# Hybrid decoder layer on one core: the token-major results and the decay chain get an earlier place in the schedule, and the decay sums become a step of their own

## The chip, the core and the metric

The kernel runs on one NeuronCore of a Trainium2 chip: TensorE (PE, with its weight loads as PEld), VectorE (DVE), ScalarE (ACT), GpSimd (POOL) and SyncE (SP, which issues the loads). Each engine takes its instructions strictly in its own order, and waits on semaphores for the other engines and for DMAs. The metric is the device time of one execution in microseconds; lower is better.

## The reference, cut to what matters

One decoder layer on 512 tokens of width 1024. One input projection feeds two mixers, a sparse attention with three gated branches and a gated DeltaNet (a recurrence with per-head decay); their outputs are merged, projected and normalised, and a convolutional MLP follows.

```
h = x @ w_in[l]
(nsa_q, cmp_k, cmp_v, slc_k, slc_v, win_k, win_v, nsa_gate,
 gdn_qkv, gdn_beta, gdn_decay, gdn_gate, merge_gate) = _split_in(h)
...
beta = jax.nn.sigmoid(beta_raw.astype(f32)).transpose(0, 2, 1)
g = (-jnp.exp(a_log.astype(f32))[None, :, None]
     * jax.nn.softplus(decay_raw.astype(f32) + dt_bias.astype(f32)).transpose(0, 2, 1))
...
gcum = jnp.cumsum(g, axis=-1)
...
mix = (jax.nn.sigmoid(gate_a) * y_a + jax.nn.sigmoid(gate_b) * y_b) @ w_o[l]
x = layer_norm(DEEPNORM_ALPHA * x + mix, ln1_g[l], ln1_b[l])
f = conv_ffn(x, ffn_w_up[l], ffn_conv_w[l], ffn_w_down[l])
x = layer_norm(DEEPNORM_ALPHA * x + f, ln2_g[l], ln2_b[l])
```

All of it is kept in float32: a product is made of three passes over operands split into a high and a low part (high by high, low by high, high by low), which is why nearly every operand has two tiles (`wh` and `wl`, `xh` and `xl`, `kh` and `kl`).

## The kernel before

**The start.** SP loads the transposed input in eight blocks of 128 channels (`xr`) and, beside them, the 288 columns of the input projection that are wanted with tokens on the partitions (`wB`: the values of two attention branches, the attention gates, beta and the decay). ACT and DVE split each block. `token_major` (L299) multiplies them block by block into four accumulators, `pb0` to `pb3`, one for each 128 tokens: 96 matmuls of 128x288. Of these accumulators ACT and DVE then take the values (`vcat`), the gates (`gsig`) and the eight columns of beta and decay (`bd`).

**The steps.** All other columns of the projection are made channel-major in pieces of 128 columns by `gemm_t`: a weight tile of 512 KB (`raw`) is loaded, split in two halves into `wh` and `wl`, and 24 matmuls of 128x512 go into a bank `gps`. There are two banks `gps`, three buffers each for `raw`, `wh` and `wl`, and the block-wise weights of `token_major` use the same `wh` and `wl` buffers. A string, `ORDER` (L128), lists the steps up to the merge. The first are `q0` (queries of the first pair of heads), `k0` (keys of the first group), `i0` (keys of the first recurrent head: product, convolution of four taps, four transposes, norms), `q1`, `j0` (queries of the first recurrent head), `m0` (its matrices) and `c` (the compressed keys and values). In what follows a product is called by its step: "q0's product" is the 24 matmuls into that step's `gps`.

**Evacuation.** `queries` (L679) empties its bank by four ACT and two DVE operations (`q`, `qf`), `keys` (L662) by four ACT (`kh`, L673) and four DVE (`kl`, L675) operations. `conv_silu` (L400) reads the bank with ACT (`acc`, L404), with DVE (L412) and, for the taps that POOL adds, with ACT again (`tap`, L409); only then is the bank free. For i0 two taps go over ACT and POOL, and POOL also makes the last two multiplications (`kq`, L420) ahead of the transposes (L426).

**The decay chain.** `decays` (L361) turns `bd` into beta and into `gdec`, the log decay: ACT makes `tb` and `se`, and DVE some thirty small operations of 128x16, each waiting for the one ahead of it (`sacc`, L382 and L383, is the longest part). Three matmuls (L394) against constant triangles make the cumulated sums, ACT takes their exponential (`eg`), DVE makes `nbe`. `gdh` and `gdl` are the split halves of `gdec` that `m0` wants (`grh`, `grl` on POOL).

**What sets the order.** The instructions are written in program order and given a priority number by a running counter; a list scheduler then sets each engine's order by these numbers and by what it reckons to be ready. `tc.high_priority(offset=n)` makes the numbers inside a block smaller (earlier) by n, and on leaving it the counter stands again where it stood on entering. The steps stand each in such a block, with an offset made of the numbers used so far (`at`) and a shift from the table `SHIFT`. So what stands inside such blocks does not move the number from which the steps count; what stands outside does. Before the change the evacuation of `token_major` and the whole of `decays` stand outside.

## Time and profile before

| | |
|---|---|
| time, median of three runs | 853.08 us (850.83 to 854.49) |
| profiled execution | span 852.4 us, from its first instruction to its last |
| PE busy | 830.1 us, 97% of the span |
| DVE / ACT / POOL busy | 597.5 / 403.6 / 160.9 us |
| mean granted TensorE clock | 0.991 |

The page gives no other time of the profiled execution than its span. A row of the timeline has the start and the length in us, the engine, the line, the operation, output and input tiles without their buffer numbers, and in brackets the idle time before it with what ended it. Matmuls are pipelined, so the distance between the starts of two rows, and not their length, is what one of them costs. "PEclk" is the clock that TensorE was granted, 1.00 being full.

### The profile page before, as it was taken

Reading aid. Unit: us, or ns where it says so; the run is one execution under the profiler, and the core shown is the slowest. Engines: PE = TensorE matmul, PEld = TensorE weight load, DVE = VectorE, ACT = ScalarE, POOL = GpSimd, SP = SyncE. Lnnn points to the kernel's source line nnn. Section 1 sums busy time; section 2 is a strip of 40 time slices with the busy share of each in tenths; the row PEclk is TensorE's granted clock in tenths of the full one; section 3 lists DMA queues with packets and bytes.
Section 4 is the critical chain, followed back from the end, with each engine's and each line's share of the span. In section 5 each row is a group of like instructions: output and inputs, shape, how many; then the busy total and the mean of one; then the engine's idle time right before and its main releaser. Section 6 shows DMA issues by size and latency. Waiting matters only on the chain.

```text
span 852.4 us, 11870 instructions
## 1 busy us (share of the span) xinstructions
PE 830.1 (97%) x4226; PEld 681.5 (80%) x4226; DVE 597.5 (70%) x1276; ACT 403.6 (47%) x890; POOL 160.9 (19%) x152
## 2 busy tenths in 40 slices
PE   8999899999999999999999999999999999999986
PEld 8777688777777788888888898888888888878864
DVE  5845579986867866674457647777777777877686
ACT  4464377575446776532234114444444444655531
POOL 0353442223136111102200003111111111100000
PEclk9999899999999999999999999999999999999998
DMA  7322111002102010254446008997966732565662
GB/s 271 86 92 99 53 48 50 25 26 75 49 27 75 26 50 25 88 181 127 124 152 219 26 1 292 253 244 236 228 206 170 198 99 86 185 210 174 203 192 99
DMA packets 35051, 108.05 MB, mean 127 GB/s; under 512 B 3248, under 2 KB 4400, under 8 KB 34608
## 3 DMA queue, kind: packets, MB, share of 16 engines
q1 hardware_dynamic: 27696, 84.23, 30.9%
q0 software_dynamic: 7296, 23.07, 11.4%
q8 instruction: 33, 0.54, 0.3%
q14 instruction: 26, 0.21, 0.1%
HBM read 105.19 MB, written 25.17 MB: 153 GB/s over the span
## 4 chain that ended last, share of the span: by engine, by line
PE 80%; DVE 11%; DMA 4%; ACT 2%; issue 2%; POOL 0%; SPq 0%; DVEq 0%; ACTq 0%; POOLq 0%
PE pu L264 9%; PE pu L262 9%; PE pu L265 9%; PE gps L262 7%; PE gps L264 7%; PE gps L265 7%; PE pout L851 2%; PE aps L834 2%; DMA raw<-wsum 2%; PE px L1136 2%; PE pw L1014 2%; PE pw L1012 2%; PE pm L265 2%; PE pm L262 2%; PE pw L1013 2%
## 5 line engine op out<-in xcount | busy, mean ns | idle before, releaser
L252 DVE TENSOR_TENSOR wl<-raw,wh 128x512 fp32r<-128x512 f32 x140 | 113.4, 811 | 67.2 <-ACT wh L248 62.8
L248 ACT ACTIVATE wh<-raw 128x512 fp32r<-128x512 f32 x136 | 85.5, 631 | 152.2 <-PE pu L264 104.2
L262 PE MATMUL pu<-mh,wh 128*128 128x512 f32 (+1 forms) x384 | 142.7, 372 | 0.0
L264 PE MATMUL pu<-ml,wh 128*128 128x512 f32 (+1 forms) x384 | 142.6, 371 | 0.0
L265 PE MATMUL pu<-mh,wl 128*128 128x512 f32 (+1 forms) x384 | 142.6, 371 | 0.0
L262 PE MATMUL gps<-xh,wh 128*128 128x512 f32 x320 | 129.7, 407 | 2.5 <-DVE xs L536 2.2
L264 PE MATMUL gps<-xl,wh 128*128 128x512 f32 x320 | 129.7, 406 | 0.0
L265 PE MATMUL gps<-xh,wl 128*128 128x512 f32 x320 | 127.8, 401 | 0.0
L262 PEld LDWEIGHTS pu<-mh,wh 128*128 128x128 f32 x384 | 72.4, 188 | 12.6
L265 PEld LDWEIGHTS pu<-mh,wl 128*128 128x128 f32 x384 | 72.4, 188 | 12.6
L264 PEld LDWEIGHTS pu<-ml,wh 128*128 128x128 f32 x384 | 72.4, 188 | 12.3
L262 PEld LDWEIGHTS gps<-xh,wh 128*128 128x128 f32 x320 | 60.8, 190 | 15.8 <-issue 2.9
L1094 DVE SCALAR_TENSOR_TENSOR fa<-pu,fcw,fa 128x511 f32<-128x511 f32 x88 | 65.7, 746 | 10.7 <-ACT fa L1091 9.2
L264 PEld LDWEIGHTS gps<-xl,wh 128*128 128x128 f32 x320 | 60.9, 190 | 11.0 <-issue 1.0
L265 PEld LDWEIGHTS gps<-xh,wl 128*128 128x128 f32 x320 | 60.9, 190 | 10.9 <-issue 0.2
L1100 POOL TENSOR_TENSOR fth<-fth,fa 128x512 f32<-128x512 f32 x22 | 28.7, 1303 | 201.5 <-DVE fa L1094 201.5
L252 POOL TENSOR_TENSOR wl<-raw,wh 128x512 fp32r<-128x512 f32 x36 | 46.3, 1288 | 93.3 <-ACT wh L248 79.2
L1071 ACT ACTIVATE wh<-raw 128x512 fp32r<-128x512 f32 x67 | 40.6, 627 | 40.9 <-DMA raw<-wsum 16.8
L1072 DVE TENSOR_TENSOR wl<-raw,wh 128x512 fp32r<-128x512 f32 x67 | 43.8, 685 | 21.0 <-ACT wh L1071 20.7
L811 ACT ACTIVATE sc<-sc,mn 128x384 f32<-128x384 f32 (+2 forms) x64 | 35.7, 559 | 12.8 <-DVE mn L809 10.6
L295 POOL TENSOR_TENSOR rs<-rs,minus_half 128x1 f32<-128x1 f32 x8 | 7.6, 946 | 170.3 <-DVE rs L973 170.3
L1091 ACT ACTIVATE fa<-pu,fcw 128x512 f32<-128x512 f32 x44 | 29.6, 672 | 10.2 <-PE pu L265 10.2
(329 smaller groups left out, 1684.0 us busy)
## 6 DMA issues: line engine op xcount, KB each, us to landing
raw<-in_up SPq DMA_DIRECT2D x44, 512.0 KB, 4.5
raw<-in_wT SPq DMA_DIRECT2D x40, 512.0 KB, 3.6
wsum<-in_down POOLq DMA_DIRECT2D x6, 2816.0 KB, 24.3
raw<-wsum SPq DMA_DIRECT2D x20, 512.0 KB, 4.3
raw<-in_down SPq DMA_DIRECT2D x15, 512.0 KB, 4.8
wsum<-wsum POOLq DMA_DIRECT2D x2, 2816.0 KB, 12.5
raw<-in_wm SPq DMA_DIRECT2D x8, 512.0 KB, 3.7
raw<-in_wo SPq DMA_DIRECT2D x8, 512.0 KB, 3.6
```

Of the source, the lines that this page charges most:

```text
L248: A.activation(wh, r, AF.Copy)
L252: eng.tensor_tensor(wl, r, wh.bitcast(F32), op=OP.subtract)
L262: i = PE.matmul(ps, wh[k], mh_(k), start=(k == 0), stop=False)
L264: PE.matmul(ps, wh[k], ml_(k), start=False, stop=False)
L265: PE.matmul(ps, wl[k], mh_(k), start=False, stop=(k == n - 1))
L811: A.activation(s[:, i, :n], s[:, i, :n], AF.Exp, scale=-1.0, bias=mn[:, 0, i:i + 1], accum_out=mn[:, 1, i:i + 1])
L834: PE.transpose(pt[:, i, k, :], s[:, i, k * 128:(k + 1) * 128], ident)
L1071: A.activation(hi, raw[:, i], AF.Copy)
L1072: V.tensor_tensor(lo, raw[:, i], hi.bitcast(F32), op=OP.subtract)
L1091: A.activation(acc, ps, AF.Copy, scale=w[:, 2:3])
L1094: V.scalar_tensor_tensor(acc[:, n:], ps[:, :S - n], w[:, i:i + 1], acc[:, n:], op0=OP.mult, op1=OP.add)
L1100: G.tensor_tensor(th, th, g[1], op=OP.mult)
```

## The change

Three edits. The evacuation of the token-major accumulators moves into a block with priority 600 numbers earlier, and the four copies of `bd` come ahead of the values and gates. `decays` moves into such a block as well, and loses its tail. That tail (the three matmuls of the sums, the exponential and `nbe`) becomes `decay_sums`, a step `d` between `k0` and `i0` without an entry in `SHIFT`. No instruction is added or removed.

```diff
 LATE = 2500
+EARLY = 600
...
-ORDER = "q0 k0 i0 q1 j0 m0 c n0 w0 i1 j1 v0 v1 p0 o0 a0 y0 b0 a1 b1 m1 a2 b2 n1 w1 i2 j2 o1 y1 m2 v2 a3 n2 q2 w2 b3 o2 y2 q3 g0 p1 k1 i3 j3 a4 b4 m3 a5 n3 w3 g1 g2 b5 v3 o3 a6 g3 b6 a7 g4 b7 g5 y3".split()
+ORDER = "q0 k0 d i0 q1 j0 m0 c n0 w0 i1 j1 v0 v1 p0 o0 a0 y0 b0 a1 b1 m1 a2 b2 n1 w1 i2 j2 o1 y1 m2 v2 a3 n2 q2 w2 b3 o2 y2 q3 g0 p1 k1 i3 j3 a4 b4 m3 a5 n3 w3 g1 g2 b5 v3 o3 a6 g3 b6 a7 g4 b7 g5 y3".split()
...
-        for t in range(TT):
-            ps = pss[t]
-            hi = vcat[:, t, :, :, 0, :]
-            src = ps[:, :256].rearrange("p (a b c) -> p a b c", a=2, b=2)
-            A.activation(hi, src, AF.Copy)
-            V.tensor_tensor(vcat[:, t, :, :, 1, :], src, hi.bitcast(F32), op=OP.subtract)
-            A.activation(gsig[:, t, :], ps[:, 256:280], AF.Tanh, scale=0.5)
-            A.activation(bd[:, t, :], ps[:, 280:288], AF.Copy)
-        V.tensor_scalar(gsig, gsig, 0.5, 0.5, op0=OP.mult, op1=OP.add)
+        with tc.high_priority(offset=EARLY):
+            for t in range(TT):
+                A.activation(bd[:, t, :], pss[t][:, 280:288], AF.Copy)
+            for t in range(TT):
+                ps = pss[t]
+                hi = vcat[:, t, :, :, 0, :]
+                src = ps[:, :256].rearrange("p (a b c) -> p a b c", a=2, b=2)
+                A.activation(hi, src, AF.Copy)
+                V.tensor_tensor(vcat[:, t, :, :, 1, :], src, hi.bitcast(F32), op=OP.subtract)
+                A.activation(gsig[:, t, :], ps[:, 256:280], AF.Tanh, scale=0.5)
+            V.tensor_scalar(gsig, gsig, 0.5, 0.5, op0=OP.mult, op1=OP.add)
...
         V.tensor_tensor(gdl, gdec, gdh.bitcast(F32), op=OP.subtract)
+
+    def decay_sums():
         ps = dps()
         gv = gdec.rearrange("p a b -> p (a b)")
...
-    decays()
+    with tc.high_priority(offset=EARLY):
+        decays()
...
-             "i": gdn_k, "j": gdn_q, "v": gdn_v, "m": gdn_mid, "n": gdn_tri, "w": gdn_inv, "y": gdn_gate,
+             "d": decay_sums, "i": gdn_k, "j": gdn_q, "v": gdn_v, "m": gdn_mid, "n": gdn_tri, "w": gdn_inv, "y": gdn_gate,
```

All that the engines' orders show of the change lies in the first 100 us of the program. Three places carry the prediction. Line numbers after the change are higher by one to six.

**SP, the front of the program** (`raw_391` is the weight tile of q0, `xr0` the first input block, `wB0` the first columns). Before:

```order
L1240 UNCONDITIONAL_BRANCH
L214 DMA xr0_122<-in_xT 128x256
L216 DMA wB0_130<-in_wB 128x288
L214 DMA xr0_122<-in_xT 128x256
L214 DMA xr1_123<-in_xT 128x256
```

After:

```order
L1246 UNCONDITIONAL_BRANCH
L242 DMA raw_391<-in_wT 128x1024
L215 DMA xr0_122<-in_xT 128x256
L217 DMA wB0_130<-in_wB 128x288
L215 DMA xr0_122<-in_xT 128x256
```

The load of q0's weights, which stood behind all input blocks, is now the first load of the program, and every input block stands one place later in the queue.

**PE, the end of the token-major product** (`pb3` is the fourth accumulator, `gps_407` and `gps_401` q0's product, `gps_451` and `gps_445` k0's, `gps_497` i0's, before and after). Before:

```order
L265 MATMUL gps_407<-xh_93,wl_405 128x512
L311 MATMUL pb0_118<-wh_279,xl_94 128x288
L309 MATMUL pb1_119<-wh_279,xh_93 128x288
L310 MATMUL pb1_119<-wl_280,xh_93 128x288
L311 MATMUL pb1_119<-wh_279,xl_94 128x288
L309 MATMUL pb2_120<-wh_279,xh_93 128x288
L310 MATMUL pb2_120<-wl_280,xh_93 128x288
L311 MATMUL pb2_120<-wh_279,xl_94 128x288
L309 MATMUL pb3_121<-wh_279,xh_93 128x288
L310 MATMUL pb3_121<-wl_280,xh_93 128x288
L311 MATMUL pb3_121<-wh_279,xl_94 128x288
L262 MATMUL gps_451<-xh_93,wh_443 128x512
```

After:

```order
L263 MATMUL gps_497<-xh_93,wh_493 128x512
L265 MATMUL gps_497<-xl_94,wh_493 128x512
L266 MATMUL gps_497<-xh_93,wl_495 128x512
L312 MATMUL pb3_121<-wh_279,xl_94 128x288
L266 MATMUL gps_445<-xh_93,wl_443 128x512
L263 MATMUL gps_445<-xh_93,wh_441 128x512
L265 MATMUL gps_445<-xl_94,wh_441 128x512
L266 MATMUL gps_445<-xh_93,wl_443 128x512
```

The last token-major matmul, which stood between q0's product and k0's, now stands behind the whole of i0's product, ahead of the last seven matmuls of k0's. The ten token-major matmuls before it are strewn among those of k0 and i0. The three matmuls of the decay sums, which stood among the last three matmuls of k0's product, now stand behind j0's product, round the transposes of i0.

**ACT and DVE, the evacuation of i0 and k0 and the decay chain** (`acc_522`, `tap_525` and `tap_528` empty i0's bank; `wh_602` is the first half of j0's weights; `kh` and `kl` empty k0's bank). ACT before:

```order
L404 ACTIVATE acc_522<-gps_497,tiny_317 128x512
L409 ACTIVATE tap_525<-gps_497,tiny_317 128x510
L409 ACTIVATE tap_528<-gps_497,tiny_317 128x509
L395 ACTIVATE eg_335<-dps_391 128x48
L673 ACTIVATE kh_476<-gps_451 64x512 x2
L248 ACTIVATE wh_602<-raw_600 128x512
```

ACT after:

```order
L409 ACTIVATE acc_522<-gps_497,tiny_317 128x512
L315 ACTIVATE bd_106<-pb3_121 128x8
L320 ACTIVATE vcat_104<-pb3_121 128x4x64
L367 ACTIVATE tb_352<-bd_106 128x16
L249 ACTIVATE wh_602<-raw_600 128x512
L414 ACTIVATE tap_525<-gps_497,tiny_317 128x510
L414 ACTIVATE tap_528<-gps_497,tiny_317 128x509
L375 ACTIVATE se_358<-say_359 128x16
```

DVE before, the end of the chain:

```order
L388 SCALAR_TENSOR_TENSOR gdec_332<-sacc_368,ea_386 128x16
L412 SCALAR_TENSOR_TENSOR acc_522<-gps_497,tiny_317,acc_522 128x511
L389 CAST gdh_333<-gdec_332 128x16
L390 TENSOR_TENSOR gdl_334<-gdec_332,gdh_333 128x16
L396 SCALAR_TENSOR_TENSOR nbe_336<-beta_331,eg_335 128x16
L675 TENSOR_TENSOR kl_477<-gps_451,kh_476 64x512 x2
```

DVE after, the middle of the chain:

```order
L385 TENSOR_TENSOR sacc_368<-sacc_368,sz2_366 128x16
L680 TENSOR_TENSOR kl_471<-gps_445,kh_470 64x512
L386 TENSOR_SCALAR sacc_368<-sacc_368 128x16
L680 TENSOR_TENSOR kl_471<-gps_445,kh_470 64x512
L253 TENSOR_TENSOR wl_604<-raw_600,wh_602 128x512
L385 TENSOR_TENSOR sacc_368<-sacc_368,sz2_366 128x16
```

On ACT the first half of j0's weights moved from behind i0's taps and k0's first copies to ahead of the taps, together with the last `bd` and `vcat`. On DVE the chain was closed before k0's low parts (`kl`) and j0's weights (`wl_604`); now i0's first convolution step stands ahead of the chain, and the chain runs round the `kl` operations and on behind `wl_604`.

## The prediction

> **What bounds the kernel now.** I read the page first, then PE's waits, then the stretches round them.
>
> ```profile
> span 852.4 us, 11870 instructions
> PE 830.1 (97%) x4226; PEld 681.5 (80%) x4226; DVE 597.5 (70%) x1276; ACT 403.6 (47%) x890; POOL 160.9 (19%) x152
> ...
> PE gps L262 <- DVE xs L536: 2.2, 1, 2.2
> PE dps L394 <- DVE gdec L388: 1.6, 1, 1.6
> ...
> PE pb L309 <- ACT wh L233: 1.0, 1, 1.0
> ...
> PE gps L262 <- ACT qf L689: 0.3, 1, 0.3
> ```
>
> PE is busy for 97% of the span, and of its few waits one is the change's target: the matmuls of the decay sums (L394) wait 1.6 us for `gdec`. The stretches show a second cost behind it (columns: stretch, length, busy time and instructions of PE, PEld, DVE, ACT, POOL, granted clock, DMA share, GB/s):
>
> ```profile
> 5.00:9.20 4.20, 3.21 (x24) 2.86 (x22) 1.85 (x4) 1.95 (x5) 0.00 (x0) 1.00 0.91 268
> 9.20:17.00 7.80, 7.67 (x55) 7.33 (x55) 6.38 (x14) 4.82 (x10) 0.00 (x0) 1.00 1.03 402
> ...
> 35.80:38.00 2.20, 0.55 (x4) 0.23 (x3) 1.93 (x10) 0.00 (x0) 0.00 (x0) 1.00 0.00 0
> 38.00:42.30 4.30, 4.30 (x16) 3.20 (x16) 2.87 (x6) 3.17 (x6) 3.93 (x4) 0.62 0.18 23
> ...
> 93.30:100.00 6.70, 6.49 (x25) 5.82 (x26) 1.98 (x4) 2.85 (x5) 3.18 (x3) 0.52 0.01 2
> ```
>
> After the wait the granted clock is 0.62 for 4.3 us, which loses (1 - 0.62) x 4.3 = 1.6 us of PE work. So this wait costs 1.6 + 1.6 = 3.2 us. The wait of 2.2 us for `xs`, which ends at 93.3, is followed by 6.7 us at 0.52, another 3.2 us; the 1.0 us of L309, between 5 and 9.2, costs no clock. So a wait of about 1.6 us is enough to slow the clock, one of 1.0 us is not.
>
> The rows of PE that carry the sum:
>
> ```profile
> 28.60 0.50 PE L262 MATMUL gps<-xh,wh 128*128 128x512 f32 x1 [0.28 <-ACT qf L689]
> ...
> 35.54 0.39 PE L264 MATMUL gps<-xl,wh 128*128 128x512 f32 x1
> 35.77 0.39 PE L265 MATMUL gps<-xh,wl 128*128 128x512 f32 x1
> 37.80 0.37 PE L394 MATMUL dps<-gdec,cst 128*128 128x16 f32 x2 [1.65 <-DVE gdec L388]
> ...
> 38.33 0.29 PE L394 MATMUL dps<-gdec,cst 128*128 128x16 f32 x2
> ...
> 39.60 0.76 PE L262 MATMUL gps<-xh,wh 128*128 128x512 f32 x1
> ...
> 46.91 0.39 PE L265 MATMUL gps<-xh,wl 128*128 128x512 f32 x1
> ...
> 51.91 0.60 PE L426 MATMUL dps<-ident,kq 128*128 128x128 f32 x4
> ...
> 52.81 0.40 PE L265 MATMUL gps<-xh,wl 128*128 128x512 f32 x1
> ...
> 57.69 0.33 PE L426 MATMUL dps<-ident,kq 128*128 128x128 f32 x1
> ```
>
> i0's product begins at 28.60, the sums at 37.80, q1's product at 39.60, the third matmul of j0's product is at 46.91, i0's transposes at 51.91, the third matmul of c's first product at 52.81 and j0's transposes at 57.69. A matmul of 128x512 costs 0.23 us at full clock (35.54 to 35.77).
>
> **Part one: the weight load at the front.** The token-major matmuls need the input blocks as early as they can come.
>
> ```profile
> 0.73 0.39 SPq L214 DMA_DIRECT2D xr<-in_xT  x1
> ...
> 4.01 4.71 DMA wB<-in_wB
> ...
> 16.64 0.36 DVE L250 CAST wh<-raw 128x512 fp32r<-128x512 f32 x1
> ...
> 24.95 0.29 PE L310 MATMUL pb<-wl,xh 128*128 128x288 f32 x1
> 25.08 0.29 PE L311 MATMUL pb<-wh,xl 128*128 128x288 f32 x1
> ```
>
> The chain of waits runs through this start: the columns of the third block, issued at 4.01, land after 4.71 us, at 8.7, and PE waits for their split. Now 512 KB stand ahead of all blocks. At the 402 GB/s of the stretch from 9.2 to 17 they take 524288 / 402000 = 1.3 us; that is the upper bound. The DMA engines were 0.91 busy from 5 to 9.2, so a queue that is never empty can win back at most 9% of the 8.0 us from 0.73 to 8.7, 0.7 us; that gives 0.6 as the lower bound. I take **+1.0**, between them. No gain is possible, as the tile is first read at 16.64, long after it landed in its old place. After 9.2 PE runs without a gap (7.67 of 7.80 us), so the delay is carried on whole.
>
> [...]
>
> **Part two: from i0's product to q1's.** The times below leave the +1.0 out; it is added at the end.
>
> ```profile
> 24.59 1.21 ACT L316 ACTIVATE vcat<-pb 128x256 fp32r<-128x256 f32 x4
> ...
> 34.38 0.69 ACT L404 ACTIVATE acc<-gps,tiny 128x512 f32<-128x512 f32 x1 [3.25 <-PE gps L265]
> 38.24 1.26 ACT L409 ACTIVATE tap<-gps,tiny 128x510 f32<-128x510 f32 x2 [3.17 <-DVE acc L412]
> 39.68 1.19 ACT L673 ACTIVATE kh<-gps 64x512 fp32r<-64x512 f32 x2
> 40.89 0.63 ACT L248 ACTIVATE wh<-raw 128x512 fp32r<-128x512 f32 x1
> ...
> 32.41 1.15 DVE L380 TENSOR_SCALAR sacc<-sz 128x16 f32<-128x16 f32 x1
> ...
> 36.33 0.17 DVE L383 TENSOR_SCALAR sacc<-sacc 128x16 f32<-128x16 f32 x1
> 36.53 0.17 DVE L382 TENSOR_TENSOR sacc<-sacc,sz 128x16 f32<-128x16 f32 x1
> ...
> 40.90 1.38 DVE L675 TENSOR_TENSOR kl<-gps,kh 64x512 fp32r<-64x512 f32 x2 [0.23 <-ACT kh L673]
> ```
>
> i0's start still hangs on the last copy of q0's bank, whose chain is as long as before, so it stays at 28.6. From there PE has 34 matmuls of 0.23 (all 24 of i0, ten of k0) and four token-major ones of 0.13 (24.95 to 25.08): 8.3 us, to 36.9. i0's last matmul is the 29th of these, at 35.1. q1's product takes i0's bank, and its start waits for the taps: ACT does `acc` (0.69, from 35.5), the last `bd`, `vcat` and `tb` (0.30 for one `vcat`, the small ones estimated at 0.2 each), then `wh_602`, whose buffer is freed only by k0's last but one matmul at about 37.0 (0.63), and the two taps (1.26): 38.9. Behind the waiting `wh_602` stand the taps, `se` and `kh`, and PE and DVE wait for them. So PE waits from 37.2 to 38.9, **1.7 us in place of the 1.6** that were there; the new wait is for taps, not for `gdec`. q1 starts 0.7 earlier than the 39.60 of before, since the sums no longer stand ahead of it.
>
> **Part three: to j0's product.** It takes k0's bank and needs all four `kl`, and its third matmul `wl_604`. `kh` begins when ACT is through with the taps and `se`, at 39.2, and the pairs take 1.2 each. Before, four `kl` (0.69 each) ran behind a closed chain. Now ten `sacc` operations of 0.2 and the chain's start stand among them: chain from 39.2 to 41.2 (seven links, with half a microsecond for one as slow as the 1.15 above), two `kl` to 42.8, seven operations to 44.3, two `kl` to 45.9, `wl_604` (about 0.7) to 46.6. PE would have ended q1 at 38.9 + 24 x 0.23 = 44.4 at full clock, or 46.0 after another slow stretch. Either way j0's third matmul is at 46.7 against 46.91: **the 0.7 shrinks to 0.2**, and the slow clock costs nothing there because DVE's chain ends later.
>
> **Part four: i0's transposes and c.**
>
> ```profile
> 38.37 1.05 POOL L487 TENSOR_TENSOR grh<-cst,gdh 128x512 fp32r<-128x512 f32 x1 [3.58 <-DVE gdh L389]
> ...
> 46.90 1.28 POOL L420 TENSOR_TENSOR kq<-th,acc 128x512 f32<-128x512 f32 x1
> 48.12 0.61 POOL L250 CAST wh<-raw 128x512 fp32r<-128x512 f32 x1
> 48.81 1.29 POOL L252 TENSOR_TENSOR wl<-raw,wh 128x512 fp32r<-128x512 f32 x1
> ...
> 57.62 0.16 DVE L459 TENSOR_TENSOR gk<-gk,nbe 128x4 f32<-128x4 f32 x1
> ```
>
> The nine last links of the chain follow `wl_604`, so `gdh` is there at 48.3, ten us later than before. POOL's order now has `grh` and `grl` (1.05 each) ahead of `kq` (1.28): `kq` is done at 51.7, where before it was at 48.2. PE ends j0 at 46.7 + 22 x 0.23 = 51.8, so the transposes stand at 51.9, as before. Then come the three sums, 0.4 us at full clock (they show 0.29 at the slow one), which PE paid earlier before. c's `wh` and `wl` follow `kq` on POOL (0.61 + 1.29): 53.7, and c's third matmul waits 0.3 for it: **53.75 against 52.81, +0.9**. Twenty more matmuls lead to j0's transposes. `grl` is ready at 50.4, well ahead of the matmul behind them; `nbe` comes near 54 and is read at 57.62. Both are hidden with 3 us and more; without that cover the ten us that the chain lost would show.
>
> The values and gates, moved along with `bd`, are first read by the attention steps behind c and cost nothing.
>
> **Sum.** +1.0 + 0.9 = +1.9 on the profiled span: 852.4 + 1.9 = **854.3**. Behind 60 us PE is the bound again and passes the delay on; the wait for `xs` starts and ends with PE's own order. The profiled execution lies 0.7 under the median of 853.08, within the 3.7 us that the runs differ.
>
> **The rivals.** *The change does what it says*: the wait and its slow clock go, no wait comes in their place: 852.4 - 3.2 + 1.0 = 850.2. For it speaks that q1's wait (1.7) stands close to the 1.6 from which the clock is known to fall, and is made of many short rows; against it, that the order has `wh_602` ahead of the taps and the last token-major matmul behind i0. *Slower, by the clock*: the waits at q1 and at j0 each slow the clock after j0 has begun, for as long as the 6.7 us behind the wait for `xs`: +3.2, 857.5. It decides if the second wait comes out at 1.6 or more; my walk has 1.4. [...] *Nothing else moves*: the load costs its lower bound, and what q1 wins covers what c loses: 852.4 + 0.6 = 853.0.
>
> **How the numbers follow.** The forecast has 0.55, the first rival 0.2, the slower one 0.13, the last 0.12. A difference under 0.5% (4.3 us) is about what a measurement of this kernel can't tell from no change. Faster than 848.1 needs the first rival and more, a third of it: 0.07. Slower than 856.7 is the clock's rival with hardly more than its middle, some of the forecast's tail: 0.13. Within 0.5%: 0.8. The forecast's own range is 853.6 (0.6 at the front and no wait at c) to 855.6 (1.3 at the front, and one more link of DVE's chain at 1.15 in place of 0.2). The wide one takes in the first rival and most of the slower one: 850.0 to 857.3.
>
> **What would show it.** In the changed profile: the first `xh` on ACT about 1 us later and PE's first gap longer; no wait of L399 for `gdec`; a wait of q1's first matmul for `tap` near 38 to 40; `kl` at 46 to 47 ahead of j0; `kq` near 52. The prediction is wrong if PE has no wait between 36 and 48, if the front is not late, or if the slow clock shows twice before 60 us.

## The result, and the profile after

The changed kernel takes 858.35 us (median of 13 runs, 854.76 to 861.18) against 854.27 us (13 runs, 849.91 to 857.08) of the kernel before beside it: a ratio of 1.0056, 95% interval 1.0039 to 1.0073. The prediction had 854.3 us and a range up to 857.3; the time lies above both.

The profiled execution is one of the quickest of the 13: its span is 853.0 us and its time 854.77. In all runs of the layer that list both, the time is 1.7 to 1.9 us above the span.

The page of the changed kernel begins as follows; the counts of the five engines are those of before:

```profile
span 853.0 us, 11868 instructions
...
PE 827.7 (97%) x4226; PEld 678.6 (80%) x4226; DVE 599.3 (70%) x1276; ACT 402.8 (47%) x890; POOL 162.0 (19%) x152
```

PE is busy for 97% of the span, so that only a few waits are left to look at. The three longest are (engine, tile and line, what it waited for, us in total, times, longest):

```profile
PE gps L263 <- DVE kl L680: 3.7, 1, 3.7
PE gps L263 <- DVE xs L541: 2.2, 1, 2.2
PE gps L263 <- ACT tap L414: 1.7, 1, 1.7
```

The wait for `gdec` is gone, a wait of 1.7 us for `tap` stands where the prediction put it, and a wait of 3.7 us for `kl` is the longest of the program. PE's timeline of the changed kernel has the places (line numbers moved by one to five against the kernel before):

```profile
10.31 0.40 PE L310 MATMUL pb<-wh,xh 128*128 128x288 f32 x1 [1.01 <-ACT wh L234]
...
29.47 0.50 PE L263 MATMUL gps<-xh,wh 128*128 128x512 f32 x1 [0.21 <-ACT qf L694]
...
40.12 0.47 PE L263 MATMUL gps<-xh,wh 128*128 128x512 f32 x1 [1.69 <-ACT tap L414]
...
49.49 0.47 PE L263 MATMUL gps<-xh,wh 128*128 128x512 f32 x1 [3.65 <-DVE kl L680]
...
63.10 0.33 PE L431 MATMUL dps<-ident,kq 128*128 128x128 f32 x1
```

i0 starts 0.87 us later than before (29.47 against 28.60), q1 0.52, j0 3.0 (its first matmul stood at 46.46), j0's transposes 5.4 (63.10 against 57.69). The whole loss is made by then. Around the long wait the stretches read (columns as in the prediction):

```profile
45.80:49.50 3.70, 0.05 (x2) 0.04 (x1) 3.40 (x10) 2.55 (x5) 1.26 (x1) 1.00 0.00 0
49.50:56.80 7.30, 7.30 (x26) 5.63 (x27) 4.90 (x13) 1.82 (x4) 5.02 (x5) 0.77 0.25 74
```

PE stands still for 3.7 us, and the clock behind it is 0.77 for 7.3 us, 1.7 us of PE work. What DVE does meanwhile, in its timeline from the end of i0's convolution on:

```profile
38.12 1.01 DVE L368 TENSOR_SCALAR hbeta<-tb 128x16 f32<-128x16 f32 x1
39.04 0.16 DVE L369 TENSOR_SCALAR beta<-tb 128x16 f32<-128x16 f32 x1
39.12 1.24 DVE L371 TENSOR_TENSOR sy<-bd,tiny 128x16 f32<-128x16 f32 x1
40.28 0.41 DVE L321 TENSOR_TENSOR vcat<-pb,vcat 128x256 fp32r<-128x256 f32 x1
40.62 0.99 DVE L374 SCALAR_TENSOR_TENSOR say<-sy 128x16 f32<-128x16 f32 x1
41.90 1.09 DVE L377 TENSOR_SCALAR sz<-se 128x16 f32<-128x16 f32 x1 [0.28 <-ACT se L375]
...
44.03 0.68 DVE L680 TENSOR_TENSOR kl<-gps,kh 64x512 fp32r<-64x512 f32 x1
...
47.72 0.90 DVE L386 TENSOR_SCALAR sacc<-sacc 128x16 f32<-128x16 f32 x1
48.65 0.69 DVE L680 TENSOR_TENSOR kl<-gps,kh 64x512 fp32r<-64x512 f32 x1
```

and POOL's timeline beside it:

```profile
37.82 2.51 POOL L253 TENSOR_TENSOR wl<-raw,wh 128x512 fp32r<-128x512 f32 x2
40.29 2.66 POOL L415 TENSOR_TENSOR acc<-acc,tap 128x510 f32<-128x510 f32 x2
47.33 1.26 POOL L424 TENSOR_TENSOR th<-th,acc 128x512 f32<-128x512 f32 x1 [4.38 <-ACT th L420]
```

A link is here one small operation of the decay chain, which needs the one ahead of it. Five links of 128x16 that take 0.17 or 0.18 us in the kernel before, in rows where POOL rests, take 0.9 to 1.24 here, and each ends where a POOL instruction ends: `hbeta` at 39.13 (POOL's first `wl` at 39.09), `sy` at 40.36 (the second at 40.33), `say` at 41.61 and `sz` at 42.99 (the two adds at 41.58 and 42.95), `sacc` at 48.62 (`th` at 48.59). `vcat` (0.41 us at 40.28, beside the first of the two adds) and `kl` (0.69 at 46.99, the third of the four, beside `th`), which read a PSUM bank, keep their length: before, a `vcat` takes 0.42 and a `kl` 0.69. The same stands in the kernel before, whose rows the prediction took for one slow link. POOL's timeline before:

```profile
31.53 0.62 POOL L250 CAST wh<-raw 128x512 fp32r<-128x512 f32 x1 [11.17 <-PE gps L264]
32.23 1.30 POOL L252 TENSOR_TENSOR wl<-raw,wh 128x512 fp32r<-128x512 f32 x1
```

The `sacc` of 1.15 us at 32.41 ended at 33.56; POOL's `wl` ended at 33.53.

**Two parts of a time.** The runs of one kernel differ by 6 us and more, and so do their listed clocks. Span times mean granted clock is about what the span would be at full clock, as PE is busy nearly throughout (97%); span less that is what the clock took. Over the timed runs of each kernel (mean, with its standard error):

| kernel | runs | span | at full clock | lost to the clock |
|---|---|---|---|---|
| before, beside e1 to e4 | 23 | 851.1 | 844.9 ±0.4 | 6.3 ±0.6 |
| before, beside e5 to e8 | 25 | 850.5 | 844.4 ±0.2 | 6.1 ±0.4 |
| before, beside e9 to e11 | 16 | 849.4 | 844.5 ±0.3 | 4.9 ±0.6 |
| before, beside e12 to e14 | 28 | 851.0 | 845.2 ±0.2 | 5.8 ±0.5 |
| the changed kernel | 13 | 856.6 | 849.8 ±0.4 | 6.9 ±0.8 |

So the change costs about 5 us at full clock, and little or nothing is shown for the clock. The groups did not all run on one chip, and the kernel before alone differs by 0.8 us between them. The two profiled spans lie only 0.6 us apart because the execution of the changed kernel met the slow clock less often (0.995 against 0.991), and because its last waits (`px` and `pu`) add up to 2.8 us in place of 4.3. The wait for `xs` is 2.2 us in both profiles, but before it is followed by 6.7 us at 0.52, and after the change the clock behind it is 1.00.

### The profile page after: what moved, and what is told of

Read it like the earlier page. It is cut to its first block, busy times and chain, and to the rows that moved or that the text cites. A ratio compares the mean times of both kernels' runs of the same rounds, so it can differ in the third digit from the quotient of the medians.

```text
span 853.0 us, 11868 instructions
## 1 busy us (share of the span) xinstructions
PE 827.7 (97%) x4226; PEld 678.6 (80%) x4226; DVE 599.3 (70%) x1276; ACT 402.8 (47%) x890; POOL 162.0 (19%) x152
## 4 chain that ended last, share of the span: by engine, by line
PE 77%; DVE 13%; DMA 4%; ACT 3%; issue 2%; POOL 1%; SPq 0%; DVEq 0%; ACTq 0%; POOLq 0%
PE pu L263 9%; PE pu L266 9%; PE pu L265 9%; PE gps L263 7%; PE gps L265 6%; PE gps L266 6%; PE pout L856 2%; DVE wl L1078 2%; PE aps L839 2%; DMA raw<-in_down 2%; PE px L1142 2%; PE pw L1018 2%; PE pw L1019 2%; PE pm L265 2%; PE pm L263 2%
```

## The experiments

Theory A: the loss is a side effect. Instructions that move into a `high_priority` block no longer count in the number from which the steps are counted, so the steps come 53 numbers earlier (by the code 48 from i0 on, as `d` counts five of its own), and the order that results is bad. Theory B: the three edits cost the time as written. Theory C: it is only the clock. Later, on why `kl` is late: theory L (DVE is held up by POOL's instructions) against theory O (the chain merely stands ahead of `kl`).

| run | time, us | ratio to before, 95% | at full clock | lost to the clock |
|---|---|---|---|---|
| e1, counter put right | 853.56 | 1.0003 (0.9981 to 1.0024) | 845.4 ±0.4 | 6.0 |
| e2, load back, counts drift | 888.52 | 1.0412 (1.0385 to 1.0438) | | |
| e3, sums alone | 854.32 | 1.0007 (0.9990 to 1.0025) | 845.1 ±0.3 | 6.9 |
| e4, splits off POOL | 862.04 | 1.0095 (1.0065 to 1.0125) | 849.8 ±0.3 | 9.5 |
| e5, load first, alone | 854.38 | 1.0018 (1.0000 to 1.0037) | 845.2 ±0.3 | 6.8 |
| e6, load back, alone | 855.50 | 1.0050 (1.0030 to 1.0071) | 845.9 ±0.4 | 8.9 |
| e7, POOL still | 856.79 | 1.0049 (1.0028 to 1.0071) | 848.8 ±0.3 | 5.9 |
| e9, before with PSUM | 855.10 | 1.0047 (1.0027 to 1.0067) | 847.3 ±0.3 | 5.8 |
| e10, after with PSUM | 861.58 | 1.0131 (1.0107 to 1.0155) | 852.2 ±0.5 | 7.9 |
| e11, e1 with PSUM | 860.44 | 1.0107 (1.0073 to 1.0141) | 849.0 ±0.3 | 8.9 |
| e12, before with PSUM, second way | 849.94 | 0.9974 (0.9953 to 0.9994) | 843.2 ±0.2 | 5.1 |
| e13, after with PSUM, second way | 857.24 | 1.0051 (1.0029 to 1.0072) | 849.9 ±0.4 | 5.7 |
| e14, e1 with PSUM, second way | 851.09 | 0.9980 (0.9958 to 1.0001) | 844.1 ±0.3 | 5.5 |

**e1: the counter put right.**

```diff
-    at = 0
+    at = 53
     for step in ORDER:
```

> The three edits are kept, but the steps get back the 53 priority numbers that they lost when the decay chain's instructions left the step counter (the counter starts at 53 in place of 0). The order that results has the first query's weight load behind the input blocks again, no token-major matmul between i0's, and the decay chain on DVE ahead of i0's convolution. Theory A (the loss comes from the side effect: the load at the front, about 1.1 us, and the chain that meets POOL's work and makes kl late, 3.65 us of wait and a slow clock behind it) expects no wait of 3.65 us for kl, PE's second token-major matmul at about 9.2 us, and a time below the kernel before by 1.6 to 3 us (ratio 0.996 to 0.999). Theory B (the loss lies in the edits as written: chain ahead of kl on DVE, early token-major results) expects kl late all the same and a ratio of 1.003 to 1.006. Theory C (the difference is only in which clock windows a run happens to meet) expects a ratio within 0.999 to 1.002 with the same waits.

The load stands behind the input blocks again, and the loss is gone: 1.0003. But nothing is won either. PE's timeline of e1:

```profile
38.97 0.59 PE L263 MATMUL gps<-xh,wh 128*128 128x512 f32 x1 [2.24 <-DVE kl L680]
```

q1 now takes k0's bank and waits 2.2 us for `kl` in place of 1.65 for `gdec`. So the order that the lost numbers make is the cause of the loss, as theory A has it; its hope of a gain falls. Theory B falls: with the edits as written `kl` is still late, but the ratio is not the 1.003 to 1.006 that it expected. Theory C falls too: at full clock the changed kernel is 4.4 us above e1.

**e2: a test that tested something else.** In the changed kernel:

```diff
-        nc.sync.dma_start(out=raw, in_=src)
+        with tc.high_priority(offset=-53 if FIRST else 0):
+            nc.sync.dma_start(out=raw, in_=src)
+        FIRST.clear()
```

> The changed kernel with one thing undone: the issue of the first query's weight load gets a priority later by 53, so that it stands behind the input blocks again. In the order that results the token-major matmuls are no longer spread between i0's either, and DVE's chain is closed before kl. If the load's place is the root of both losses (theory A), PE's second token-major matmul is at 9.2 us in place of 10.3, the 3.65 us wait for kl is gone, and the ratio to before is 0.996 to 1.001; a wait of 1.5 to 2 us for i0's taps ahead of q1's product should remain, since kh stands ahead of the taps on ACT. If the load costs only its own 1.1 us and the rest comes from the edits as written (theory B), the ratio is 1.003 to 1.005.

The block took one count from every load of weights, so that the later steps drift apart, by one number more with each load. Its span of 884.5 us has new waits all over, of 5.1 us for `qf`, 3.5 for `acc`, 3.2 for `mn`, 3.0 for `z`. It says nothing of the load. It does say how much hangs on these numbers.

**e3: the sums alone.** The kernel before, with `decay_sums` as a step `d` behind `k0` and nothing else of the change.

> Only the third edit: the decay sums as a step of their own between k0 and i0; the token-major block and the chain keep the priority that they had. On PE the sums stand behind k0's last matmul in place of among its last four. If the wait for gdec (1.65 us) and the slow clock behind it are really on the path, q1's product starts 1 to 1.5 us earlier than 39.60, and the ratio is 0.996 to 0.999. If the wait only changes its name (for taps or for kl), the ratio is 0.999 to 1.001.

1.0007. PE's timeline of e3 shows the wait cut in two:

```profile
37.59 0.81 PE L397 MATMUL dps<-gdec,cst 128*128 128x16 f32 x6 [0.96 <-DVE gdec L389]
39.39 0.77 PE L263 MATMUL gps<-xh,wh 128*128 128x512 f32 x1 [0.98 <-POOL grh L490]
```

Together 1.94 us against 1.65. Behind the chain on DVE stands i0's `acc` (L415, at 37.25), behind that the taps on ACT (38.03 to 39.29), and q1's start waits for them. The releaser that the row names is `grh`, but it ended at 39.21; the taps ended last.

**e4: q1's splits off POOL.** `'wh21'` from `'G'` to `'A'` and `'ws21'` from `'G'` to `'V'` in the engine table of the changed kernel.

> The changed kernel with two entries of the engine table altered: q1's two weight splits (wh, wl) go to ACT and DVE in place of POOL. PE's and SP's order is word for word that of the changed kernel. The splits' 2.5 us on POOL at 37.8 to 40.3 are those beside which the links hbeta and sy took 1.01 and 1.24 us. Theory L (a DVE operation on SBUF alone waits for the POOL instruction that runs beside it to end) expects hbeta, beta and sy at about 0.2 us, links of about 1 us only where POOL's adds of i0's convolution run, kl's first pair earlier and j0's wait for kl at 1 to 2.5 us in place of 3.65; ratio to before 1.000 to 1.004. Theory O (the chain is late because of its place in DVE's order alone) expects j0's wait at 3.5 us or more, as DVE now has 1.4 us more work of its own, and a ratio of 1.005 or more. Both expect the 1.1 us at the front to stay.

Links where POOL now rests are short, links beside the POOL work that is left are long. DVE of e4:

```profile
39.84 0.17 DVE L368 TENSOR_SCALAR hbeta<-tb 128x16 f32<-128x16 f32 x1
...
40.00 0.16 DVE L374 SCALAR_TENSOR_TENSOR say<-sy 128x16 f32<-128x16 f32 x1
...
45.37 1.16 DVE L386 TENSOR_SCALAR sacc<-sacc 128x16 f32<-128x16 f32 x1
```

and POOL of e4:

```profile
45.17 1.32 POOL L425 TENSOR_TENSOR kq<-th,acc 128x512 f32<-128x512 f32 x1
```

The 1.16 us end at 46.53, with `kq` at 46.49. As a price it fails: DVE got the splits, j0's wait rose to 4.5 us and q1's to 2.5, and the ratio to 1.0095. Theory L had the links right, and wait and time wrong; these two are what theory O expected.

**e5: the load at the front, by itself.** In the kernel before, the first weight load gets a priority 53 numbers earlier, and the step its lost count back.

> The kernel before, with one thing taken from the changed kernel: the first query's weight load (512 KB) is issued ahead of all input blocks. The numbers of the later steps are kept (the step gets back the one count that the edit takes). PE's order stays as before but for three token-major matmuls that move behind the first query's. The prediction's first term says +1.0 us (between 0.6 and 1.3) and nothing else: PE's second token-major matmul at 10.2 to 10.4 us in place of 9.24, the wait for gdec unchanged near 1.6, and a ratio of 1.0007 to 1.0015. If the load at the front is the main part of the loss (rival), the ratio is 1.003 or more.

The matmul that the expectation calls the second token-major one (the first that needs the third block) stands at 10.16 (0.92 later), and the full-clock part is 0.8 us (with an error of 0.4) above that of the kernel before beside it. The ratio of 1.0018 lies above the expected range, which its interval takes in, and the wait at the sums is 1.2 us, less than expected. The prediction's +1.0 holds within these errors.

**e6: the changed kernel with the load back, counts kept.** The edit of e2, for the first load alone, with the count given back.

> The changed kernel with the first query's weight load behind the input blocks again, this time with the count of every later step kept (e2 took one count from each step that loads weights, so that all steps drifted apart by 1 to 12 numbers; its 35 us tell of that, and nothing of the load). In the order that results the token-major matmuls stand among k0's and few among i0's, the chain on DVE is closed ahead of kl, and the sums stand behind q1's first two matmuls. If the late chain beside POOL is what costs the changed kernel its 4 us, this kernel has no wait for kl over 1 us, a wait of 1.5 to 2.5 us for i0's taps or for gdec near 37 to 40 as before, and a ratio of 0.998 to 1.002. If the edits as written cost the time wherever the load stands, the ratio is 1.004 to 1.006.

The expectation fails: 1.0050. The wait for `kl` is gone, but the chain on DVE still ends late, now ahead of q1. PE's timeline of e6:

```profile
40.42 0.47 PE L269 MATMUL gps<-xh,wh 128*128 128x512 f32 x1 [3.06 <-DVE sacc L392]
```

In this kernel i0's `acc` waits on DVE behind eight links of `sacc` (it starts at 38.28, ACT's part of it was done at 36.7), and the taps, which end at 40.32, behind `acc`. At full clock it loses 1.5 us; with 8.9 us the clock takes 2.8 more than in the kernel before. So the chain is late with the load back as well, at another place. Against the changed kernel 3.9 us are won at full clock all the same: the load's number alone changes DVE's order too, and the wait for `kl` goes with it.

**e7: POOL still.** The changed kernel without q1's low halves and without POOL's two adds of i0's convolution.

> The changed kernel without POOL's work beside the chain: q1's low halves are left out (its product uses the high halves twice, with wrong values and the same number of matmuls), and the two adds of i0's convolution on POOL are left out. The counts of the steps are kept, and SP's order is that of the changed kernel. Theory L (a DVE operation on SBUF alone waits for the end of the POOL instruction beside it) expects hbeta, beta, sy and say at 0.16 to 0.25 us each in place of 1.0 to 1.2, links of about 1 us only where POOL's th and kq run now, j0's wait for kl at 0 to 2 us in place of 3.65, and a ratio of 1.000 to 1.003: what is left is the 1.0 us at the front and q1's wait. Theory O (the place of the chain in DVE's order alone) expects j0's wait above 3 us and a ratio of 1.004 or more.

`hbeta`, `beta`, `sy` and `say` take 0.16 or 0.17 us, as theory L had it. But POOL's `th` and `kq` move up into the gap (40.94 and 42.30, 1.29 us each), `sz` takes 1.27 and 1.05 us beside them, and j0's wait stays at 3.45. Wait and ratio are again what theory O expected; but as other links were held up in place of the first ones, it doesn't tell L from O.

**e8: two costs by themselves.** Nothing of the layer is computed. Chains of twelve links, alone and beside POOL adds; then bursts of 50 matmuls, each behind a wait for n copies on ACT:

```python
for k, (link, runs) in enumerate(((tt, False), (tt, True), (ts, False), (ts, True), (pt, False), (pt, True),
                                  (big, False), (big, True), (pbig, False), (pbig, True))):
    phase(k, link, runs)
...
for n in (1, 2, 3, 4, 5) * 6:
    ...
    for i in range(50):
        PE.matmul(ps, w, mv, start=(i == 0), stop=(i == 49))
    ...
    A.activation(t, ps, AF.Copy, scale=0.001)
    ...
```

> None of the layer is computed (the output is zero): two costs by themselves. First, ten chains of twelve dependent DVE operations, each once alone and once beside eight POOL adds of 128x512 (1.3 us each): 128x16 add of two SBUF tiles, 128x16 multiply-add of one SBUF tile, 128x16 add of a PSUM and an SBUF tile, 128x512 add of two SBUF tiles, 128x512 add of a PSUM and an SBUF tile. Theory L expects the links on SBUF alone (two inputs, or one in the fast form) to last until the POOL instruction beside them ends, about 1.2 us each in place of 0.2, and those with a PSUM input to keep their 0.2 (0.7 for 128x512). A theory of shared bandwidth expects all five forms longer by a like share, and none with its end on the end of a POOL instruction. Second, 30 bursts of 50 matmuls, with one to five copies on ACT between them (waits of some 1.5 to 4 us): if a wait of 1.6 us is enough for the slow clock, as the prediction read from two places, every burst starts with 3 to 7 us at half the clock; if only a wait that fills a window of about 3.4 us is enough, only the longest two kinds do; and if it hangs on where the wait falls in a window of fixed phase, the shorter waits show both.

DVE of e8, each form alone and then beside POOL (the second column is for all twelve):

```profile
23.44 2.47 DVE L177 TENSOR_SCALAR x<-x 128x16 f32<-128x16 f32 x12
26.87 8.26 DVE L177 TENSOR_SCALAR x<-x 128x16 f32<-128x16 f32 x12
39.38 2.47 DVE L178 TENSOR_TENSOR x<-bank,x 128x16 f32<-128x16 f32 x12
42.81 2.47 DVE L178 TENSOR_TENSOR x<-bank,x 128x16 f32<-128x16 f32 x12
54.56 8.68 DVE L179 TENSOR_TENSOR x<-x,load 128x512 f32<-128x512 f32 x12
65.39 15.44 DVE L179 TENSOR_TENSOR x<-x,load 128x512 f32<-128x512 f32 x12
82.28 8.67 DVE L180 TENSOR_TENSOR x<-bank,x 128x512 f32<-128x512 f32 x12
93.09 8.67 DVE L180 TENSOR_TENSOR x<-bank,x 128x512 f32<-128x512 f32 x12
```

On SBUF alone the chains get 3.3 and 1.8 times as long (8.26 us for 2.47, 15.44 for 8.68); with a PSUM input they don't by a hundredth (2.47 and 2.47, 8.67 and 8.67). In the chain of 8.26 us every other link is held: six take 1.12 to 1.15 us and end 0.03 us behind one of POOL's adds, and the six between them take 0.17 or 0.18, begun in the 0.08 us before POOL's next add. So not each link is held, as theory L had it, but as many as there are POOL instructions. (For the 128x16 add of two SBUF tiles POOL's adds came too late to be beside it; the changed kernel has it in `sy`, with 1.24 us, which takes 0.17 in e4, where POOL rests.) A theory of shared bandwidth expected all five forms longer by a like share, and the rows do not show that; by what means a link is held up is not shown.

PE of e8, four of the 29 waits:

```profile
19.54 11.63 PE L193 MATMUL gps<-mv,w 128*128 128x512 f32 x50 [1.35 <-ACT mv L199]
33.19 11.63 PE L193 MATMUL gps<-mv,w 128*128 128x512 f32 x50 [2.01 <-ACT mv L199]
...
79.68 13.25 PE L193 MATMUL gps<-mv,w 128*128 128x512 f32 x50 [4.00 <-ACT mv L199]
...
107.92 13.24 PE L193 MATMUL gps<-mv,w 128*128 128x512 f32 x50 [2.01 <-ACT mv L199]
```

and the stretch behind the last of them:

```profile
108.00:111.30 3.30, 3.30 (x8) 2.63 (x9) 0.00 (x0) 0.00 (x0) 0.00 (x0) 0.50 0.00 0
```

Waits of 1.35 us were followed by the slow clock in 0 of 6 cases, of 2.01 in 2 of 6, of 2.67 in 2 of 6, of 3.33 in 4 of 6, of 4.00 in 5 of 5. One rule, fitted to the starts and waits of all 29, has no exception among them: time falls into fixed windows of 3.415 us (an estimate, from these rows), the fast bursts have at most 1.8 us of idle time in any one window ahead of them and the slow ones at least 2.0, and the window behind runs at half clock, which costs a burst 1.6 us in the rows above (13.24 or 13.25 against 11.63). The two profiles of the layer have about the same length: before, the granted clock is 0.50 from 38.99 to 42.40 (3.41 us) and from 93.60 to 100.43 (6.83), and the two starts are 54.61 us apart, 16 times 3.41; after, it is 0.50 from 49.91 to 53.32 (3.41). So the third reading of the expectation holds, and no window had to be idle as a whole: waits of 2.01 us were enough in 2 of 6 cases.

**e9 to e11: the chain's values in PSUM.** The kernel before, the changed one and e1, with `bd`, `tb`, `se`, `sacc` and one copy of `sy` in the bank of the attention's output, which isn't used until then:

```diff
     pg = ps1.enter_context(tc.tile_pool(name="pg", bufs=BUFS["pg"], space=PSUM))
+    po = ps1.enter_context(tc.tile_pool(name="po", bufs=1, space=PSUM))
+    small = po.tile([128, S], F32, name="pout")
...
-        sm = lambda name: nsa.tile([128, TT, GH], F32, name=name)
+        def sm(name):
+            if name not in IN_PSUM:
+                return nsa.tile([128, TT, GH], F32, name=name)
+            i = 2 + IN_PSUM.index(name)
+            return small[:, 16 * i:16 * i + 16].rearrange("p (a b) -> p a b", a=TT)
...
```

> The kernel before, with nothing of the change, but with the decay chain's running values (bd, tb, se, one copy of sy, sacc) in a PSUM bank that is free until the attention, in place of SBUF; sy is worked out twice, so that each link reads at most one SBUF tile. e8 showed that links with a PSUM input keep their 0.21 us beside POOL. In the kernel before, three links beside POOL took 0.51, 1.15 and 0.60 us (1.7 us too long in sum) and the wait for gdec was 1.65 us. Theory L (the lock with POOL's instructions makes gdec late) expects links of 0.2 us throughout but for at most one (the square of sz, on SBUF alone), the wait for gdec under 0.5 us, q1's product 1 to 2.5 us earlier than 39.60, a full-clock part of the span (span times mean granted clock) of 842 to 843.5 in place of 844.6, and a ratio of 0.995 to 0.998. If DVE's links get longer by PSUM itself, or another wait takes the place, the ratio is 0.999 to 1.002.

> The changed kernel with the same PSUM bank for the chain's running values; counts of the steps and SP's order are those of the changed kernel. This prices the lock in the changed kernel. Theory L expects hbeta, sy and say at 0.2 us, no link of sacc over 0.3, j0's wait for kl at 0 to 1.6 us in place of 3.65, the 1.1 us at the front and q1's wait for the taps (1.5 to 2) as they are, a full-clock part of 846 to 847.5 in place of 849.8, and a ratio of 1.001 to 1.004. Theory O (the place of the chain ahead of kl) expects j0's wait above 3 us, a full-clock part of 849 or more, and a ratio of 1.005 or more.

> e1 (the three edits with the steps' counter put right) with the same PSUM bank. In e1 the wait for kl at q1's start was 2.24 us, with one link of sacc at 1.25 us beside POOL ahead of kl. Theory L expects that link at 0.2 us and the wait for kl at about 1.0 us, under the 1.7 to 2.0 us of idle time in one window from which e8's bursts went slow; a full-clock part of 843.5 to 845 and less clock lost than the 6 us of e1: ratio 0.996 to 0.999. If the order alone sets the wait, the wait stays at 2 us or more and the ratio at 0.999 to 1.002.

The links do what theory L says: in e9 all of `sacc` take 0.18 us, PE has no wait for `gdec` over 0.2, and q1 starts at 37.18. In e10 j0's wait for `kl` is 0.47 us in place of 3.65 (with 1.32 for `wl` behind it), and in e11 the wait for `kl` is 1.3 us in place of 2.24. The times do not follow, since moving the pool also changed the order somewhere else. PE of e9:

```profile
343.33 0.63 PE L436 MATMUL dps<-ident,y 128*128 128x128 f32 x4 [2.38 <-DVE y L446]
344.89 0.47 PE L265 MATMUL gps<-xh,wh 128*128 128x512 f32 x1 [0.94 <-DVE yT L668]
```

The transposes of one head's output stand ten matmuls earlier than before and wait 3.3 us in sum, in all three kernels. As tests of the price they fail.

**e12 to e14: the same with fewer values and the pool in its place.** `tb`, `se` and `sacc` only:

```diff
     po = ps1.enter_context(tc.tile_pool(name="po", bufs=1, space=PSUM))
+    small = po.tile([128, S], F32, name="pout")
...
```

> The kernel before with three of the decay chain's values (tb, se, sacc) in the PSUM bank that the attention's output uses later; bd and sy stay in SBUF and nothing is worked out twice. e9 had moved that pool ahead of the others, and with it the transposes of one head's output stood ten matmuls earlier on PE, near 343 us, with new waits of 2.4 and 0.9 us there; here PE's order differs from the kernel before only in eight matmuls around the sums. Theory L expects the links of sacc at 0.18 us, no wait for gdec, q1's product about 2 us earlier than 39.60, waits at 343 us under 0.3, a full-clock part of 842 to 843.7 in place of 844.5, and a ratio of 0.995 to 0.998. If something behind the sums gives the 2 us back, the ratio is 0.999 to 1.001.

> The changed kernel with the same three values in PSUM. The orders of PE, ACT and SP are those of the changed kernel, word for word; DVE's differs in the place of four links. sy and say stay on SBUF alone and still meet POOL's splits. Theory L: hbeta, sz and sacc at 0.2 us in place of 1.01, 1.09 and 0.90, sy and say together 1.5 to 2.2 as before; kl's last about 2 to 2.8 us earlier, so j0's wait at 0.8 to 1.7 in place of 3.65, under the 1.7 to 2.0 of idle time from which the clock goes slow; full-clock part 847 to 848 in place of 849.8, ratio 1.001 to 1.004. Theory O (the place of the chain ahead of kl alone): j0's wait above 3, full-clock part above 849, ratio 1.005 or more.

> e1 (the three edits, counter put right) with the same three values in PSUM; PE's order is that of e1, word for word. In e1 q1's start waited 2.24 us for kl, behind one link of sacc of 1.25 us. Theory L: that link at 0.2, the wait for kl at 1.0 to 1.3, a full-clock part of 844 to 845 and less clock lost than e1's 6.0 us; ratio 0.997 to 1.000. Theory O: the wait stays above 2 and the ratio within 0.999 to 1.003.

e12 is faster than both kernels, if barely clear of 1: 0.9974 (0.9953 to 0.9994), with 2.0 us less at full clock, as theory L expects. PE of e12:

```profile
37.17 0.47 PE L263 MATMUL gps<-xh,wh 128*128 128x512 f32 x1 [0.41 <-issue]
```

q1 starts 2.4 us earlier than before, and PE has no wait over 0.5 us between 9 and 60 us. But the links are not all that changed. i0's `acc` on DVE, ahead of the taps for which q1's start waits, stood behind the whole chain before and stands ahead of its last six links in e12. Before, then e12:

```profile
37.46 0.74 DVE L412 SCALAR_TENSOR_TENSOR acc<-gps,tiny,acc 128x511 f32<-128x511 f32 x1
35.03 0.75 DVE L417 SCALAR_TENSOR_TENSOR acc<-gps,tiny,acc 128x511 f32<-128x511 f32 x1 [0.34 <-ACT acc L409]
```

Six links at 0.21 us each are 1.3 us, and 0.34 of them would have gone into the time that DVE waited ahead of `acc`, so that behind them it would have begun about 0.9 us later. By this estimate some 1.5 of the 2.4 us are the hold-up and the rest is the order; no run parts the two.

e14 has 0.9980 (0.9958 to 1.0001), not clear of 1: e1's wait of 2.24 us for `kl` is down to 0.24, more than expected, and here too DVE's order differs, with 12 links of `sacc` ahead of the last `kl` in place of 17.

e13 keeps the orders of PE, ACT and SP word for word. DVE of e13:

```profile
38.06 0.17 DVE L373 TENSOR_SCALAR hbeta<-pout 128x16 f32<-128x16 f32 x1
...
38.22 0.85 DVE L376 TENSOR_TENSOR sy<-bd,tiny 128x16 f32<-128x16 f32 x1
...
39.33 0.97 DVE L379 SCALAR_TENSOR_TENSOR say<-sy 128x16 f32<-128x16 f32 x1
...
41.98 0.92 DVE L386 TENSOR_TENSOR sz<-sz 128x16 f32<-128x16 f32 x1
```

and PE of e13:

```profile
47.56 0.47 PE L264 MATMUL gps<-xh,wh 128*128 128x512 f32 x1 [1.77 <-DVE kl L685]
...
61.84 0.33 PE L436 MATMUL dps<-ident,kq 128*128 128x128 f32 x1 [0.61 <-DVE kq L432]
```

j0's wait falls from 3.65 to 1.77 us while three links on SBUF alone are still held. DVE's order differs by a little: 8 links of `sacc` stand ahead of the last `kl` in place of 11, which is 0.6 us at most. So about 1.2 us of that wait, or more, are the hold-up and not the chain's place; e10, where these links were free as well, leaves 0.47, but there the orders differed more. The time doesn't show it (1.0051 against 1.0056, full-clock parts 849.9 and 849.8), and is what theory O expected: 0.6 of the 1.9 us go to a new wait for j0's `kq`, and what is left, 1.3 us in the two traces at j0's transposes (61.84 against 63.10), is as large as the runs can tell on different chips. The price of the hold-up in the changed kernel's time is therefore not settled. In the kernel before, freeing the links together with the new place of `acc` is worth 2.0 us at full clock (e12).

What stands is this: the loss is that of the order which the lost numbers make (e1), the load at the front is 0.8 us of it (e5), and links on SBUF alone are held while POOL works (e8: twelve in 8.26 us in place of 2.47). How much of the rest is the hold-up, and how much the place of the chain, stays open.

## Why the prediction was wrong

- **Part one, the load at the front: right.** +1.0 was forecast; the trace has 1.07 (10.31 against 9.24), and e5 by itself 0.8, with an error of 0.4, at full clock.
- **Part two, to q1's product: right.** A wait of 1.7 us for the taps, q1 at 38.9 + 1.0; the trace has 1.69 and 40.12.
- **Part three, to j0's product: the step that failed.** "Chain from 39.2 to 41.2 (seven links, with half a microsecond for one as slow as the 1.15 above)" took 0.2 us for a link. Five of them took 0.9 to 1.24. Three of the five (`hbeta`, `sy`, `say`) stand ahead of `se`, where the walk has no term at all: it lets `se` follow the taps at once. They made `se` on ACT 1.6 us late, and with it `kh` and the first `kl`; `sacc` ahead of the last `kl` added 0.7, and j0's first matmul came at 49.49. With 47.7 for the third matmul the walk implied 47.2 for the first, so 2.3 us were missed. The mechanism, chain among `kl` and `kl` ahead of j0, was the one forecast; the links were mis-sized, because the long rows of the kernel before (0.51, 1.15 and 0.60 us) were read as an accident of one link and not set beside POOL's rows.
- **Part four:** the term of 0.9 at c did not occur, so that half of the forecast's +1.9 stood on a wait that never came. j0 was so late that c's `wl` was there first; the sums behind i0's transposes cost the 0.4 that was forecast (transposes +4.97 at i0, +5.41 at j0).
- **The sum.** It made a span and set it beside a median of times. Spans lie 1.7 to 1.9 us under the times, so that its own 854.3 would have been a time of 856.1. Its baseline had a further flaw: the profiled execution had lost 1.6 us of clock behind the wait for `gdec` and 3.2 behind that for `xs`, and the prediction took the first for a fixed price. It is not: runs of the same kernel at a mean clock of 0.998 lost 1.7 us to the clock in all.
- **The rivals.** "Slower, by the clock" came nearest (857.5). Its condition, a second wait of 1.6 us or more, was met with 3.65. Its price was put together differently: most of the loss is the wait itself, while the clock's share (6.9 against some 5.8 us) is within its error. "The change does what it says" fails in the changed kernel, and also in e1, where the counter is right. "Nothing else moves" (+0.6) has about the size that e1 and e3 came out at, but in neither of them does the load stand at the front, so that this is no support for it.
- **What would have shown it wrong** was named, and one of the three signs was the slow clock twice before 60 us. It showed once, behind j0's wait; the other signs (first matmuls about 1 us later, no wait for `gdec`, a wait for `tap` near 40) held. `kl` at 46 to 47 and `kq` near 52 were the two that failed: the last `kl` ended at 49.3 and `kq` at 55.5.

## What to carry to other kernels

A chain of small DVE operations beside POOL's work isn't priced by its short rows: links on SBUF alone lasted here until POOL's instruction ended (0.90 to 1.24 us in the changed kernel, 1.12 to 1.15 in e8, in place of 0.17 or 0.18), so the rows of both engines must be read side by side, and one operand in PSUM took the hold-up away (2.47 us for twelve links with POOL and without in e8, 0.17 or 0.18 for each link of `sacc` in e12). Where an order comes from running numbers, an edit that takes instructions out of the count moves every step behind it; put the count right before judging the edit (e1). Where the clock differs from run to run (0.989 to 0.998 in the kernel before), compare span times mean clock over many runs, and not two profiles.

## What was not expected of the hardware

- DVE held up until POOL's instruction ends (by 0.03 us in e8): twelve links of 128x16 on SBUF took 8.26 us in place of 2.47, with a PSUM input 2.47 in both cases. A `TENSOR_SCALAR` of `gsig` (128x96) took 0.93 us beside POOL in e13, in place of 0.21 in the kernel before, where POOL rests. The `RECIPROCAL` behind it kept its 0.24, but it began at 41.51, just as one of POOL's adds ended (41.52), where held forms run short too (0.17 or 0.18 us in e8); so it shows nothing.
- In e8 the clock fell by windows of fixed phase, 3.415 us long by the fit, from 1.8 to 2.0 us of idle time within one window on; the three stretches at half clock in the first 101 us of the two profiles are 3.41, 6.83 and 3.41 us long. Waits of 2.01 to 3.33 us in e8 were slow or not (8 of 18) by where they fell; this goes with the clock's share of 4.9 to 9.5 us in the tables, which differs from group to group. The two waits of 2.2 us for `xs` bear it out. In the profile before, half clock begins at 93.6, so that the window ahead of it (90.2 to 93.6) held the whole wait. In the profile after, half clock begins at 49.9; counted on from there, a window ends at 97.7 and parts the wait (96.5 to 98.7) into 1.2 and 1.0 us, and the clock stays at 1.00. Two things are not explained by that alone: that the wait of 1.65 us for `gdec` was enough, and that the slow stretch behind `xs` lasted two windows (93.6 to 100.4).
- Not the chip's doing but the scheduler's: a pool that was moved, with all counts kept, changed the order 300 us later (e9 to e11), for 3.3 us of wait.
